# A hybrid decoder on one core: the causal mask of a stick-breaking scan, the order of two PSUM banks and the spacing of the value transposes

## The chip, the cores and the metric

The kernel runs on one core of a Trainium2 chip. The core has a matrix engine (TensorE, in the profile PE, with its weight loads as PEld), three engines for elementwise work (VectorE or DVE, ScalarE or ACT, GpSimd or POOL), a queue (SyncE or SP) that issues the transfers between HBM and the on-chip memory SBUF, and PSUM, eight banks of 128 x 512 fp32 into which PE writes. Each engine runs its own instructions in order and waits on semaphores for the others. The metric is the device time of one launch in microseconds (us), lower is better.

## The reference

Two layers, each a gated pair of attention mixers followed by a convolutional feed-forward block, on 1024 tokens of width 1024, in fp32:

```python
def stick_breaking_attention(q, k, v):
    ...
    def block(args):
        q_blk, i = args
        z = jnp.einsum('bhqc,bhkc->bhqk', q_blk, kt).astype(jnp.float32) * scale
        qpos = i * BLOCK + jnp.arange(BLOCK)
        causal = key_pos[None, :] < qpos[:, None]
        log_stay = jnp.where(causal, jax.nn.log_sigmoid(-z), 0.0)
        later = lax.cumsum(log_stay, axis=3, reverse=True) - log_stay
        attn = jnp.where(causal, jnp.exp(jax.nn.log_sigmoid(z) + later), 0.0)
        return jnp.einsum('bhqk,bhkc->bhqc', attn, vt)
...
def reference(x, norm1, w_in, b_gate, w_br, w_o, norm2, w_up, conv_w, conv_b, w_down, norm_f):
    ...
    for l in range(DEPTH):
        h = rmsnorm(x, norm1[l])
        proj = h @ w_in[l]
        qa, ka, va, qb, kb, vb, gate_pre = jnp.split(proj, splits, axis=-1)
        ...
        o_a = dilated_mixture(hd4(qa, DSW_HEADS), hd4(ka, DSW_HEADS), hd4(va, DSW_HEADS))
        o_b = stick_breaking_attention(hd4(qb, SB_HEADS), hd4(kb, SB_HEADS), hd4(vb, SB_HEADS))
        ...
        merged = g_a * (o_a @ w_br[l, :OUT_A]) + g_b * (o_b @ w_br[l, OUT_A:])
        x = x + merged @ w_o[l]
        h2 = rmsnorm(x, norm2[l])
        ...
        x = x + (jax.nn.gelu(a, approximate=False) * v) @ w_down[l]
    return rmsnorm(x, norm_f)
```

`dilated_mixture` is softmax attention in three head groups (windows of 128, 512 and 2048 tokens, every, every fourth and every sixteenth token). In the stick-breaking part a query attends a key with the sigmoid of its score ("beta"), times the product of one minus that sigmoid ("stay") over all keys between the two. Only keys strictly ahead of the query count.

## The kernel before

**fp32 products.** PE multiplies a reduced form of fp32 (fp32r). An operand is split into a high part (a cast by ACT, L138) and the rest (a subtraction by DVE, L145), and three products of parts are added. Large products are done by blocks with seven instead of eight block products (`seven`, L1001 to L1003): `pair` takes 256 columns of the input projection through weight sums (POOL L1125 and L1134, DVE L1129 and L1135, all on the tile `in_a`), pieces `w_hi` and `w_lo`, and PSUM results `i_a`, `i_c` and `i_b`, which DVE adds up in `u` (L1161, L1167, L1175). After each of four results it calls `put(c, n, ...)`, c being which 128 columns and n which half of the tokens.

**The order.** PE's program is written out by hand: a layer's projection work (`Dense`) and its attention items are recorded in turns. `Dense` yields after each portion, called a share, half of the matmuls of one block product (six); `advance` runs some shares between the steps of attention. `dense.at(n, f)` records f once n more shares have gone by. The other engines' programs are ordered by a scheduler from dependencies and priorities.

**Stick-breaking items.** One item takes 256 queries of one head, as two rows of 128. `score` makes the scores z in PSUM, up to 512 columns at a time; ACT writes beta (L705) and stay (L706, the sigmoid with the sign turned) from them; where a block holds the diagonal, POOL sets the masked part of its last 128 columns, of beta to 0 and of stay to 1 (L709). `scans` runs over stay from the latest key to the earliest with one DVE instruction, a running product (L722: multiply by the next element, then add a column of zeros), and then multiplies beta by it, shifted by one key (L726). The blocks without the diagonal continue from the block behind them. `turn` transposes the result on PE (L734, `sb_t`), ACT and DVE split it (`sbh`, `sbl`), and `apply` multiplies it with the values (L747, `sb_o`). There are 96 scans, of which 64 hold a diagonal. Softmax items work alike: near heads at L638 and L791 to L814, far heads at L859 to L920, whose keys, queries and values are loaded from HBM (`t_kq<-tk`, `slots<-tv`).

**Values.** `pair_v` (L1217 to L1246) projects the values of a head group. Its `put` asks for a turn of the result five shares later: four PE transposes into a bank `v_t` (L1223), the cast by ACT (L1228) and the subtraction by DVE (L1229) into the only buffer of the tile `vv`, and a store to HBM (L1232 or L1234). Successive `put`s are two shares apart. `v_t` shares two PSUM banks (tag "o") with the attention results; `i_a`, `i_b` and `i_c` share another two (tag "ps").

Of the kernel before, what the change touches and what calls it, by code (L numbers as in the profile page):

```python
# [10 lines left out]
BF16 = mybir.dt.bfloat16  # L11
AF = mybir.ActivationFunctionType
ALU = mybir.AluOpType
# [3 lines left out]
P = 128  # L17
# [3 lines left out]
HF = 512  # L21
# [35 lines left out]
def f32(ap):  # L57
    return ap.bitcast(F32)
# [3 lines left out]
def trunk_kernel(ctx, tc, x, norm1, w_in, b_gate, w_br, w_o, norm2, w_up, conv_w, conv_b, w_down, norm_f, out, depth=None, probe=None):  # L62
    nc = tc.nc
    act, dve, pe, pool = nc.scalar, nc.vector, nc.tensor, nc.gpsimd
# [3 lines left out]
    cp = ctx.enter_context(tc.tile_pool(name="cp", bufs=1))  # L68
    sb = ctx.enter_context(tc.tile_pool(name="sb", bufs=1))
    ps = ctx.enter_context(tc.tile_pool(name="ps", bufs=2, space=PSUM))  # L70
# [8 lines left out]
    pool.memset(eps, EPS)  # L79
    zero = cp.tile([P, 1], F32, name="zero")  # L80
    pool.memset(zero, 0.0)
    base0 = cp.tile([P, 256], BF16, name="base0")
    base2 = cp.tile([P, 256], BF16, name="base2")

# [2 lines left out]
    def masks():  # L87

        t = [sb.tile([P, 256], F32, tag="pt", bufs=PT, name=f"msk{i}") for i in range(3)]
        pool.iota(t[1], [[-1, 256]], base=P, channel_multiplier=1, allow_small_or_imprecise_dtypes=True)  # L90
        pool.affine_select(t[1], t[1], [[-1, 256]], ALU.is_ge, FAR, base=P, channel_multiplier=1)
        pool.affine_select(t[2], t[1], [[1, 256]], ALU.is_ge, FAR, base=0, channel_multiplier=-1)
        dve.tensor_copy(base0, t[2])
        rem = sb.tile([P, 256], I32, tag="pt", bufs=PT, name="rem")
        pool.iota(rem, [[-1, 256]], base=256, channel_multiplier=1)
        one = dve.tensor_scalar(rem, rem, 3, None, ALU.bitwise_and)
        tc.add_manual_dep(one.ins, LAST["g0"], NO_SYNC, reason="in turn")
        dve.tensor_copy(t[0], rem)
        dve.tensor_scalar(t[0], t[0], FAR, None, ALU.mult)
        LAST["base"] = dve.tensor_tensor(base2, t[1], t[0], ALU.add).ins.name  # L100
# [18 lines left out]
    sv = [dr.tile([P, n, KD, P], F32, name=f"sv{n}") for n in (4, 2, 2)]  # L119
    dn = [dr.tile([4, T], F32, name=f"dn{i}") for i in range(2)]  # L120

    def bank(tag, name):
        return ps.tile([P, 512], F32, tag=tag, name=name)

    def small(name, dtype=F32):
        return sb.tile([P, 512], dtype, tag="pt", bufs=PT, name=name)
# [510 lines left out]
    def scores(o, qt, ql, k):  # L637
        pe.matmul(o, qt, k, start=True, stop=False, skip_group_check=True)  # L638
        pe.matmul(o, ql, k, start=False, stop=True, skip_group_check=True)
# [48 lines left out]
    def stick_item(dense, u, qp):  # L688
        q, k, v = R["slots"][:, qp], R["kv"][:, 0, :], R["kv"][:, 1, :]
        pr, s = divmod(u, 2)  # L690
        rows, st, shared, left = {}, {}, {}, []

        def score(a):
            L = P * (2 * qp + a + 1)
            bt = rows[a] = sb.tile([P, T], F32, tag="p4", bufs=4, name="beta")
            if a == 0:
                st[0] = sb.tile([P, 2, T], F32, tag="xa", bufs=4, name="stay")
            sv = st[0][:, a, :]
            for c1 in range(L, 0, -512):
                c0 = max(0, c1 - 512)  # L700
                w = c1 - c0
                z = bank("s", "z")
                scores(z[:, :w], *(q[:, x, a * P : a * P + P] for x in range(2)), k[:, c0:c1])
                with tc.high_priority(offset=AHEAD):
                    act.activation(bt[:, c0:c1], z[:, :w], AF.Sigmoid)  # L705
                    act.activation(sv[:, c0:c1], z[:, :w], AF.Sigmoid, scale=-1.0)  # L706
                    if c1 == L:
                        for x, fill in ((bt, 0.0), (sv, 1.0)):
                            pool.affine_select(x[:, L - P : L], x[:, L - P : L], [[-1, P]], ALU.is_gt, fill, base=0, channel_multiplier=1)  # L709
                (SCANS if c1 == L else left).append((shared, bt, sv, c0, c1, L))  # L710
            if a:
                SCANS.extend(left)
                dense.rows += 1
                scans(2)

        def scans(most):

            while SCANS and most:
                most -= 1
                _, bt, sv, c0, c1, L = SCANS.pop(0)  # L720
                rev = sv[:, c0:c1][:, ::-1]
                one = dve.tensor_tensor_scan(rev, rev, zero[:, 0:1].to_broadcast([P, c1 - c0]), 1.0 if c1 == L else sv[:, c1 : c1 + 1], ALU.mult, ALU.add)  # L722
                if "dve" in LAST:
                    tc.add_manual_dep(one.ins, LAST["dve"], NO_SYNC, reason="in turn")
                k0, k1 = max(0, c0 - 1), c1 - 1
                dve.tensor_tensor(bt[:, k0:k1], bt[:, k0:k1], sv[:, k0 + 1 : k1 + 1], ALU.mult)  # L726

        def turn(kb):
            while any(x[0] is shared and x[4] > kb * P for x in SCANS):
                scans(1)  # L730
            tp = bank("t", "sb_t")
            todo = [(j, a) for j in range(2) for a in range(2) if kb + j <= 2 * qp + a]
            for c, (j, a) in enumerate(todo):
                pe.transpose(tp[:, c * P : c * P + P], rows[a][:, (kb + j) * P : (kb + j + 1) * P], ident)  # L734
            shared[kb] = parts(tp, len(todo) * P, "sb")
            scans(2)

        def apply(kb):
            first = kb == 2 * qp
            if first:  # L740
                shared["o"] = bank("o", "sb_o")[:, :256]
                dense.free[qp] = u + 1
            o = shared["o"]
            for j in range(2):
                c = P if first and j else 0
                for p in (0, 1):
                    pe.matmul(  # L747
                        o[:, c:256],
                        v[:, (kb + j) * P : (kb + j + 1) * P],
                        shared[kb][p][:, 256 * j : 256 * j + 256 - c],  # L750
                        start=(first and j == 0 and p == 0),
                        stop=(kb == 0 and j == 1 and p == 1),
                        skip_group_check=True,
                    )
            if kb == 0:
                out_ = small("ob")[0:64, 0:256]
                fold(out_, o)
                nc.sync.dma_start(obd[64 * s : 64 * s + 64, pr, qp * 256 : (qp + 1) * 256], out_)

        sc = [lambda: score(0), lambda: score(1)]  # L760
        return sc, [(lambda kb=kb: turn(kb), lambda kb=kb: apply(kb)) for kb in range(2 * qp, -2, -2)]

# [337 lines left out]
    def pair(dense, l, offs, tiled, put):  # L1100
# [12 lines left out]
        for c in range(2):  # L1113
            one = nc.sync.dma_start(
                raw[:, 2 * c : 2 * c + 2, :].rearrange("p a (k n) -> p (a k) n", n=P),
                w_in[l][:, offs[c] : offs[c] + P].rearrange("(k p) n -> p k n", p=P),
            )
# [20 lines left out]
        u = sb.tile([P, T], F32, tag="wr", bufs=NRAW, name="u")  # L1138
        u1, u2 = u[:, HF:T], u[:, 0:HF]
        u5 = small("u5")  # L1140
        pa, pc = bank("ps", "i_a"), bank("ps", "i_c")
        yield from seven(pa, w1, half(1, 0), True, True)
        yield
        with tc.high_priority(offset=AHEAD):
# [72 lines left out]
    def pair_v(dense, l, g):  # L1217


        def turn(c, n, f):  # L1220
            tp = bank("o", "v_t")
            for r in range(4):
                pe.transpose(tp[:, r * P : (r + 1) * P], f[:, r * P : (r + 1) * P], ident)  # L1223
            tw = tp.rearrange("p (r h c) -> p r h c", r=4, h=2)
            vv = sb.tile([P, 2, 4, P], F32R, tag="ot", name="vv")
            wv = vv.rearrange("p h r c -> p r h c")
            with tc.high_priority(offset=AHEAD):
                act.copy(wv[:, :, :, 0:64], tw)  # L1228
                dve.tensor_tensor(wv[:, :, :, 64:128], tw, f32(wv[:, :, :, 0:64]), ALU.subtract)  # L1229
            if g:  # L1230
                there = tv[c][:, :, :, g - 1, n * P : (n + 1) * P].rearrange("h r p c -> p (h r) c")
                nc.sync.dma_start(there, f32(vv).rearrange("p h r c -> p (h r) c"))  # L1232
            else:
                nc.sync.dma_start(sv[1 + c][:, :, 4 * n : 4 * n + 4, :], f32(vv))  # L1234
            if (c, n) == (1, 1):
                dense.done |= {f"v{g}"} if g else {f"V{u}" for u in range(4, 8)}

        def put(c, n, x, psum, room=None):
            f = x
            if psum:  # L1240
                f = small("vf")
                act.copy(f.rearrange("p (r j) -> p r j", r=4) if g else f, x)
            dense.at(5, lambda: turn(c, n, f))

        off = OFF_VA + 256 * g
        return pair(dense, l, (off, off + P), g > 0, put)  # L1246
# [893 lines left out]
```

## Time and profile before

| | us |
|---|---|
| median of 3 runs | 2643.26 |
| lowest and highest run | 2641.87, 2645.58 |
| the profiled execution | 2641.53 |
| its span, from first to last instruction | 2639.8 |
| PE busy | 2610.7 |
| DVE busy | 2069.4 |
| ACT busy | 1346.8 |
| POOL busy | 685.7 |

How to read it: "L722" is line 722 of the kernel printed above. A timeline row gives the start and the duration in us, the engine, line and operation, what is written from what, the shapes and, in square brackets, how long the engine stood idle just before and what released it. A row with "xN" joins N instructions that follow one another. A row of waits gives "engine, first tile, line <- what ended the wait: total us, times, longest us". A row of a group gives the total busy time, the mean time of one in ns, and after the bar the idle time of the engine just ahead of that group and what ended it. A row of windows gives the window, its length, and then for each engine (PE, PEld, DVE, ACT, POOL) its busy time and the number of instructions, the granted PE clock, the share of the DMA engines and GB/s. Layer 0's attention lies between about 80 and 560 us of the span, layer 1's between about 1380 and 1900.

### The profile page before, as it was taken

Reading aid. Unit: us, or ns where it says so; the run is one execution under the profiler, and the core shown is the slowest. Engines: PE = TensorE matmul, PEld = TensorE weight load, DVE = VectorE, ACT = ScalarE, POOL = GpSimd, SP = SyncE. Lnnn points to the kernel's source line nnn. Section 1 sums busy time; section 2 is a strip of 40 time slices with the busy share of each in tenths; the row PEclk is TensorE's granted clock in tenths of the full one; section 3 lists DMA queues with packets and bytes.
Section 4 is the critical chain, followed back from the end, with each engine's and each line's share of the span. In section 5 each row is a group of like instructions: output and inputs, shape, how many; then the busy total and the mean of one; then the engine's idle time right before and its main releaser. Section 6 shows DMA issues by size and latency. Waiting matters only on the chain.

```text
span 2639.8 us, 36722 instructions
## 1 busy us (share of the span) xinstructions
PE 2610.7 (99%) x12732; PEld 2182.9 (83%) x12732; DVE 2069.4 (78%) x3110; ACT 1346.8 (51%) x2500; POOL 685.7 (26%) x588
## 2 busy tenths in 40 slices
PE   9999999999999999999999999999999999999999
PEld 8888888888888888888888888888888888888887
DVE  7877776785888898896677778677858898888865
ACT  6655566574554555422445555656645555554225
POOL 3222110131143344321222221101321343334200
PEclk9999999999999999999999999999999999999999
DMA  7433587873244444688344436787632444457862
GB/s 253 148 120 128 150 218 197 219 255 88 81 152 149 154 156 148 237 318 315 144 145 144 128 124 174 200 222 217 207 99 82 161 147 156 141 170 259 339 239 111
DMA packets 400423, 468.26 MB, mean 177 GB/s; under 512 B 24309, under 2 KB 315501, under 8 KB 398445
## 3 DMA queue, kind: packets, MB, share of 16 engines
q1 hardware_dynamic: 400220, 465.90, 55.0%
q8 instruction: 101, 1.65, 0.3%
q14 instruction: 86, 0.70, 0.1%
q10 hardware_dynamic: 16, 0.00, 0.0%
HBM read 303.23 MB, written 162.59 MB: 176 GB/s over the span
## 4 chain that ended last, share of the span: by engine, by line
PE 85%; DVE 8%; issue 2%; ACT 2%; DMA 2%; POOL 0%; SPq 0%; DVEq 0%; ACTq 0%; POOLq 0%
PE u_a L1001 5%; PE u_a L1003 5%; PE u_a L1002 5%; PE d_ps L1755 4%; PE d_ps L1757 4%; PE d_ps L1756 4%; PE i_a L1001 4%; PE i_a L1003 4%; PE i_a L1002 4%; PE u_c L1001 3%; PE u_c L1003 3%; PE u_c L1002 3%; PE o_ps L179 2%; PE o_ps L181 2%; PE o_ps L180 2%
## 5 line engine op out<-in xcount | busy, mean ns | idle before, releaser
L145 DVE TENSOR_TENSOR w_lo<-up_a,w_hi 128x512 fp32r<-128x512 f32 x240 | 237.4, 995 | 20.6 <-ACT w_hi L138 20.6
L138 ACT CAST w_hi<-up_a 128x512 fp32r<-128x512 f32 x240 | 149.3, 622 | 184.3 <-PE u_a L1002 45.4
L138 ACT CAST w_hi<-in_a 128x512 fp32r<-128x512 f32 x252 | 156.3, 622 | 159.5 <-PE i_a L1002 58.0
L145 DVE TENSOR_TENSOR w_lo<-in_a,w_hi 128x512 fp32r<-128x512 f32 x252 | 182.8, 727 | 60.9 <-ACT w_hi L138 58.4
L1763 DVE TENSOR_TENSOR x<-x,d_ps 128x512 f32<-128x512 f32 (+1 forms) x228 | 151.9, 671 | 78.2 <-PE d_ps L1757 77.0
L1494 POOL TENSOR_TENSOR cv<-cv 128x512 f32<-128x512 f32 x88 | 132.3, 1515 | 249.6 <-DVE cv L1489 139.8
L145 DVE TENSOR_TENSOR g<-cv,g 128x512 fp32r<-128x512 f32 x154 | 151.9, 988 | 5.2 <-ACT g L138 2.7
L1755 PE MATMUL d_ps<-gd_in,w_hi 128*128 128x512 f32 (+1 forms) x340 | 130.5, 384 | 1.7 <-issue 0.8
L1134 POOL TENSOR_TENSOR in_a<-in_a 128x512 f32<-128x512 f32 x36 | 49.6, 1377 | 314.5 <-DVE w_lo L145 290.2
L1757 PE MATMUL d_ps<-gd_in,w_lo 128*128 128x512 f32 (+1 forms) x340 | 129.8, 382 | 0.0
L1756 PE MATMUL d_ps<-gd_in,w_hi 128*128 128x512 f32 (+1 forms) x340 | 129.8, 382 | 0.0
L1001 PE MATMUL u_a<-hh,w_hi 128*128 128x512 f32 x320 | 124.6, 389 | 0.8 <-DVE u L1645 0.7
L1003 PE MATMUL u_a<-hh,w_lo 128*128 128x512 f32 x320 | 124.5, 389 | 0.0
L1002 PE MATMUL u_a<-hl,w_hi 128*128 128x512 f32 x320 | 124.5, 389 | 0.0
L1001 PE MATMUL u_a<-t_hi,w_hi 128*128 128x512 f32 x320 | 124.5, 389 | 0.0
L1003 PE MATMUL u_a<-t_hi,w_lo 128*128 128x512 f32 x320 | 124.5, 389 | 0.0
L1002 PE MATMUL u_a<-t_lo,w_hi 128*128 128x512 f32 x320 | 124.5, 389 | 0.0
L1001 PE MATMUL i_a<-hh,w_hi 128*128 128x512 f32 x288 | 119.2, 414 | 0.0
L722 DVE TENSOR_TENSOR_SCAN stay<-stay,zero 128x512 f32<-128x512 f32 (+2 forms) x96 | 101.2, 1066 | 22.2 <-POOL stay L709 22.2
L1001 PE MATMUL i_a<-t_hi,w_hi 128*128 128x512 f32 x288 | 118.5, 412 | 0.0
L138 ACT CAST g<-cv 128x512 fp32r<-128x512 f32 x154 | 95.0, 617 | 38.2 <-POOL cv L1494 29.5
L1755 PE MATMUL d_ps<-gd_in,wd 128*128 128x512 f32 (+1 forms) x292 | 113.9, 390 | 0.0
(384 smaller groups left out, 8373.5 us busy)
## 6 DMA issues: line engine op xcount, KB each, us to landing
gd<-g SPq DMA_DIRECT2D x154, 512.0 KB, 3.5
gd_in<-gd SPq DMA_DIRECT2D x154, 512.0 KB, 5.7
up_a<-in_w_up_dram SPq DMA_DIRECT2D x80, 512.0 KB, 4.9
in_a<-in_w_in_dram SPq DMA_DIRECT2D x72, 512.0 KB, 5.6
wd_raw<-in_w_down_dram SPq DMA_DIRECT2D x22, 1024.0 KB, 11.5
gin<-gs SPq DMA_DIRECT2D x32, 512.0 KB, 4.0
w_raw<-in_w_o_dram SPq DMA_DIRECT2D x64, 256.0 KB, 2.9
gs<-u SPq DMA_DIRECT2D x48, 256.0 KB, 3.4
```

What stands on the lines that cost most here:

```text
L138: one = act.copy(hi, src)
L145: two = dve.tensor_tensor(lo, src, f32(hi), ALU.subtract)
L179: pe.matmul(o, lh, rh, start=(first and i == 0), stop=False, skip_group_check=share)
L722: one = dve.tensor_tensor_scan(rev, rev, zero[:, 0:1].to_broadcast([P, c1 - c0]), 1.0 if c1 == L else sv[:, c1 : c1 + 1], ALU.mult, ALU.add)
L1001: pe.matmul(o, w[0][:, c], rh, start=(first and i == 0), stop=False, skip_group_check=True)
L1002: pe.matmul(o, w[0][:, c], rl, start=False, stop=False, skip_group_check=True)
L1003: pe.matmul(o, w[1][:, c], rh, start=False, stop=(last and i == 3), skip_group_check=True)
L1494: return lambda: pool.tensor_tensor(dst, a, b, ALU.subtract)
L1755: pe.matmul(o[:, sub], wh[:, c], gh[:, sub], start=(i == 0 and k in (0, 4, 5)), stop=False, skip_group_check=True)
L1756: pe.matmul(o[:, sub], wh[:, c], gl[:, sub], start=False, stop=False, skip_group_check=True)
L1757: pe.matmul(o[:, sub], wl[:, c], gh[:, sub], start=False, stop=(i == m - 1), skip_group_check=True)
L1763: dve.tensor_tensor(x, x, o[:, sub], ALU.add)
```

## The change

Three edits, none of which changes what is computed:

1. A constant tile `over` of 128 x 512 bf16 is made once: zero, and in its last 128 columns one where the mask applies. Scans of blocks that hold the diagonal take `over` (its last columns, reversed like stay) as their second operand with the maximum in place of the addition, so that the running product is one at masked keys. POOL's select on stay goes; the one on beta remains.
2. In `pair` the PSUM tiles `i_c` and `i_a` are asked for in the other order.
3. The turn of `put(c, n)` comes 4 + c + 2n shares later instead of five: 4, 5, 6 and 7 shares for the four calls, in the order in which they come.

```diff
@@ -79,6 +79,7 @@
     zero = cp.tile([P, 1], F32, name="zero")
     pool.memset(zero, 0.0)
+    over = cp.tile([P, 512], BF16, name="over")
@@ -91,6 +92,8 @@
         dve.tensor_copy(base0, t[2])
+        pool.memset(over, 0.0)
+        pool.affine_select(over[:, HF - P : HF], over[:, HF - P : HF], [[-1, P]], ALU.is_gt, 1.0, base=0, channel_multiplier=1)
         rem = sb.tile([P, 256], I32, tag="pt", bufs=PT, name="rem")
@@ -705,8 +708,7 @@
                     if c1 == L:
-                        for x, fill in ((bt, 0.0), (sv, 1.0)):
-                            pool.affine_select(x[:, L - P : L], x[:, L - P : L], [[-1, P]], ALU.is_gt, fill, base=0, channel_multiplier=1)
+                        pool.affine_select(bt[:, L - P : L], bt[:, L - P : L], [[-1, P]], ALU.is_gt, 0.0, base=0, channel_multiplier=1)
@@ -719,7 +721,10 @@
                 rev = sv[:, c0:c1][:, ::-1]
-                one = dve.tensor_tensor_scan(rev, rev, zero[:, 0:1].to_broadcast([P, c1 - c0]), 1.0 if c1 == L else sv[:, c1 : c1 + 1], ALU.mult, ALU.add)
+                if c1 == L:
+                    one = dve.tensor_tensor_scan(rev, rev, over[:, HF - (c1 - c0) : HF][:, ::-1], 1.0, ALU.mult, ALU.max)
+                else:
+                    one = dve.tensor_tensor_scan(rev, rev, zero[:, 0:1].to_broadcast([P, c1 - c0]), sv[:, c1 : c1 + 1], ALU.mult, ALU.add)
@@ -1138,7 +1143,7 @@
-        pa, pc = bank("ps", "i_a"), bank("ps", "i_c")
+        pc, pa = bank("ps", "i_c"), bank("ps", "i_a")
@@ -1240,7 +1245,7 @@
-            dense.at(5, lambda: turn(c, n, f))
+            dense.at(4 + c + 2 * n, lambda: turn(c, n, f))
```

## The prediction

> **What bounds the kernel now.** I read the page's totals first, then the waits of TensorE (PE), then the groups of the lines that the diff touches, and last the timeline around each PE stall that such a line can reach.
>
> ```profile
> span 2639.8 us, 36722 instructions
> PE 2610.7 (99%) x12732; PEld 2182.9 (83%) x12732; DVE 2069.4 (78%) x3110; ACT 1346.8 (51%) x2500; POOL 685.7 (26%) x588
> ```
>
> PE is busy for 2610.7 of 2639.8 us, so only 29.1 us of the span is idle PE. No edit removes a matmul: the PE program keeps its 12732 instructions. Whatever the change brings must come out of those 29.1 us, and only out of the waits that end on a touched line or on work queued behind one:
>
> ```profile
> PE sb_t L734 <- DVE beta L726: 3.2, 3, 1.7
> PE i_c L1001 <- DVE kq_l L594: 3.0, 2, 1.5
> PE v_t L1223 <- DVE vv L1229: 2.7, 3, 1.7
> ...
> PE z L638 <- DMA slots<-tv: 1.1, 1, 1.1
> ...
> PE z L638 <- DVE st L791: 0.7, 1, 0.7
> ...
> DVE stay L722 <- POOL stay L709: 22.2, 26, 2.0
> ```
>
> The columns are total us, times, longest. The scans' 22.2 us behind Pool's mask look like the prize, but that is idle time of DVE, which is idle for some 570 us anyway; PE pays only where it waits for a scan's successor, L726, or for DVE work queued behind it. The first three rows, 8.9 us, and the last PE row, 0.7 us, are what the edits can reach: 9.6 us is the ceiling of the gain, 0.36% of the span.
>
> **Edit 1, the mask.** It removes 64 Pool selects on stay and makes 64 of the 96 scans read `over` and take the maximum.
>
> ```profile
> L709 POOL TENSOR_SCALAR_AFFINE_SELECT stay<-stay 128x128 f32<-128x128 f32 x64 | 27.1, 423 | 5.1 <-ACT stay L706 4.4
> L722 DVE TENSOR_TENSOR_SCAN stay<-stay,zero x96: 411/1209/2312, 81.0 to 1624.6; 128x512 f32<-128x512 f32 x48, 128x384 f32<-128x384 f32 x16, 128x128 f32<-128x128 f32 x16, 128x256 f32<-128x256 f32 x16
> ```
>
> Pool loses 27.1 us of its 685.7, which no end hangs on. The scan: 411 ns for the narrowest form (128 columns) and about 1209 for 512 give (1209 - 411) / 384 = 2.08 ns a column. The price of `over` in place of a broadcast column is not in the trace. From below: nothing (before, too, the scan reads two operands from SBUF), and no gain, since the number of columns is the same. From above, two nearby rows:
>
> ```profile
> 3.78 0.28 DVE L93 CAST base<-msk 128x256 bf16<-128x256 f32 x1
> ...
> 5.03 0.42 DVE L100 TENSOR_TENSOR base<-msk,msk 128x256 bf16<-128x256 f32 x1
> ...
> 242.13 1.28 POOL L1125 TENSOR_TENSOR in_a<-in_a 128x512 f32<-128x512 f32 x1
> 242.20 2.30 DVE L722 TENSOR_TENSOR_SCAN stay<-stay,zero 128x512 f32<-128x512 f32 x1 [0.54 <-POOL stay L709]
> ```
>
> A second full operand costs (0.42 - 0.28) / 256 = 0.55 ns a column, 0.28 us a 512-wide scan; far out, a scan takes 2.30 us when a Pool tensor_tensor has started just before it, 1.09 more than 1.21. I take nothing: 0.55 ns a column of operand reading fits inside the 2.08 that the scan spends anyway. [...]
>
> Where the earlier start reaches PE, site by site. Site A (twice, once a layer):
>
> ```profile
> 207.11 0.59 ACT L706 ACTIVATE stay<-z 128x512 f32<-128x512 f32 x1
> ...
> 207.77 0.29 POOL L709 TENSOR_SCALAR_AFFINE_SELECT stay<-stay 128x128 f32<-128x128 f32 x1
> ...
> 208.10 1.22 DVE L722 TENSOR_TENSOR_SCAN stay<-stay,zero 128x512 f32<-128x512 f32 x1 [2.01 <-POOL stay L709]
> ...
> 212.89 0.77 DVE L726 TENSOR_TENSOR beta<-beta,stay 128x512 f32<-128x512 f32 x1
> ...
> 213.71 0.44 PE L734 MATMUL sb_t<-ident,beta 128*128 128x128 f32 x2 [0.73 <-DVE beta L726]
> ...
> 1516.61 0.44 PE L734 MATMUL sb_t<-ident,beta 128*128 128x128 f32 x2 [0.73 <-DVE beta L726]
> ```
>
> ScalarE's sigmoid ends at 207.70, the select lets the scan go at 208.06: the scan gains 0.36. From 208.10 to the end of L726 at 213.66 DVE's rows name no idle time, so the whole chain moves: -0.36 of 0.73, twice, -0.7 us. Site D, the third wait for L726:
>
> ```profile
> 1381.26 1.29 POOL L1125 TENSOR_TENSOR in_a<-in_a 128x512 f32<-128x512 f32 x1
> ...
> 1382.59 0.76 DVE L1129 TENSOR_TENSOR in_a<-in_a 128x512 f32<-128x512 f32 x1 [1.45 <-POOL in_a L1125]
> 1383.27 1.30 DVE L722 TENSOR_TENSOR_SCAN stay<-stay,zero 128x512 f32<-128x512 f32 x1
> ...
> 1388.27 0.44 PE L734 MATMUL sb_t<-ident,beta 128*128 128x128 f32 x2 [1.68 <-DVE beta L726]
> ```
>
> Here the built order changes: the scan now stands ahead of L1129, so it may begin while DVE waits for Pool's 1381.26 operation. It then runs beside that operation, as at 242.20, and ends about 1.2 us behind 1382.55, at 1383.8; L1129 follows and the chain behind both is some 0.2 us earlier: -0.2 of the 1.68. Bounds: all 1.68 back, or 1.1 lost.
>
> Site C is a stretch in which DVE never rests, and PE waits at its end:
>
> ```profile
> 277.70:296.40 18.70, 17.22 (x89) 14.08 (x87) 18.70 (x28) 8.01 (x16) 3.83 (x4) 1.00 0.23 87
> ...
> 277.70:296.40 18.70, 5.71 (x6) 1.00 0.23 87
> ...
> 276.87 1.29 POOL L1125 TENSOR_TENSOR in_a<-in_a 128x512 f32<-128x512 f32 x1
> ...
> 277.70 1.01 DVE L145 TENSOR_TENSOR w_lo<-in_a,w_hi 128x512 fp32r<-128x512 f32 x1 [0.95 <-ACT w_hi L138]
> ...
> 291.80 0.68 DVE L145 TENSOR_TENSOR w_lo<-in_a,w_hi 128x512 fp32r<-128x512 f32 x1
> ...
> 296.36 0.50 PE L1001 MATMUL i_c<-t_hi,w_hi 128*128 128x512 f32 x1 [1.48 <-DVE kq_l L594]
> ...
> 1600.07 0.50 PE L1001 MATMUL i_c<-t_hi,w_hi 128*128 128x512 f32 x1 [1.49 <-DVE kq_l L594]
> ```
>
> In the first row, of a window, the third busy time is DVE: 18.70 of 18.70; the second is the same window for L722 alone, six scans. Work that starts no earlier than the window cannot shorten it, but its first operation took 1.01 where the same form takes 0.68, beside Pool's 276.87 operation. Without the stay selects ahead of it Pool starts that operation about 0.6 us earlier and is out of the way: -0.3, in both layers -0.6 us. Bounds: nothing, or the full 3.0.
>
> The new tile costs a Pool memset and select once, at the start.
>
> ```profile
> 405.09 0.52 POOL L857 MEMSET t_kq<- 64x512 f32 x1 [12.97 <-PE o L814]
> ...
> 6.05 0.16 DVE L1976 RECIPROCAL ss<-ss 128x1 f32<-128x1 f32 x1 [0.60 <-ACT ss L1975]
> ```
>
> That is 0.52 plus a 128x128 select of about 0.3; they stand ahead of the mask's iota, whose product DVE uses, and DVE has 0.60 idle before its first work on the path. Nothing; without that cover, 0.8. Edit 1: -1.5 us.
>
> **Edit 2, the banks.** The two tiles share a tag of two banks, and a bank is taken at first use, which is `i_a` in both texts. The built programs with and without this edit are the same in every instruction, wait and bank: nothing, with no bounds to keep.
>
> **Edit 3, the turns.** Four transposes a turn move: first turn a share earlier, second unmoved, third one and fourth two shares later, 24 turns in all. ACT, DVE and one store on SP's queue follow each. Nothing is added. The stall that it is aimed at:
>
> ```profile
> 238.39 0.60 PE L1223 MATMUL v_t<-ident,u 128*128 128x128 f32 x4
> ...
> 242.03 0.60 PE L1223 MATMUL v_t<-ident,u 128*128 128x128 f32 x4
> ...
> 244.96 0.59 ACT L1228 CAST vv<-v_t 128x512 fp32r<-128x512 f32 x1 [0.69 <-DMA sv<-vv]
> ...
> 246.34 0.68 DVE L1229 TENSOR_TENSOR vv<-v_t,vv 128x512 fp32r<-128x512 f32 x1
> ...
> 247.17 0.63 PE L1223 MATMUL v_t<-ident,vf 128*128 128x128 f32 x4 [0.87 <-DVE vv L1229]
> ...
> 1550.85 0.63 PE L1223 MATMUL v_t<-ident,vf 128*128 128x128 f32 x4 [1.66 <-DVE vv L1229]
> ```
>
> The single `vv` buffer holds up ACT until the store before it has landed, DVE empties the bank late, and PE waits in the fourth turn. The second and third turns (238.39 and 242.03) stand two shares apart, so two shares are 3.6 us of PE work, more than either stall: -0.87 - 1.66 = -2.5 us. The third wait on L1229 (2.7 less 2.53: 0.2) and the 0.7 us on L791 lie in one stretch of layer 0,
>
> ```profile
> 409.45 0.39 PE L638 MATMUL z<-kv,slots 128*128 128x256 f32 x1 [0.73 <-DVE st L791]
> ```
>
> where the fourth turn's copy on ACT now falls among `w_hi`, `p0h` and the exponentials: 0.9 freed, 0.6 given back by a 0.59 copy ahead of one of them, -0.3. The moved store on SP goes behind two value loads of the far heads; PE's only wait on such a load (`slots<-tv`, 1.1) is for a later one and stays. Bounds of edit 3: nothing, or -3.4.
>
> **The sum.** -0.7 - 0.2 - 0.6 - 2.5 - 0.3 = -4.3 us. The profiled execution took 2641.53 us, 1.7 outside its span; it would take 2637.2. The median of the runs lies 1.7 above it, so the forecast is 2643.26 - 4.3 = 2638.9 us.
>
> **The rivals.** *More comes free* (26%): DVE's starts ahead of sites C and D move so that their waits go too, -6 to -9.6 us, about 2636. For it: each scan that lost 0.36 at A lost the same elsewhere. Against: site C is full from its first operation. *Edit 3 is absorbed* (12%): the later copies hold up ACT's queue, or the wait on the store turns up at the third turn, which moves one share only; -2.5 and -0.3 go, edit 1 stays: 2641.8. *The second operand is dear* (12%), the one on the slower side: in site C six scans at +1.09, twice, are at most 13.1; at A and D two each, three times, 6.5; less 4.3, so 2643.26 + 15.3 = 2658.6. It decides from about 0.24 us a scan (18 scans, 4.3 us), slightly under the 0.28 of the lower row. Against: both rows are of other operations or of a collision. [...] *It doesn't do what it says*: for edit 2 that is the case, at no cost.
>
> **How the numbers follow.** The forecast has 50%, with its own range of 2637 to 2641. A difference under 0.2%, 5.3 us, can't be told from none here. Faster than 2638.0: the 26% and 6% from the forecast's lower edge, 32%. Slower than 2648.5: the 12%. The rest is no change, 56%. The range runs from 2633 (9.6 under the median, rounded) to 2648, which takes in a scan dearer by up to 0.5 us and leaves out the rival's far end.
>
> **What would show it.** Scans of 128x512 at 1.21 us beside `over`; DVE's wait of 22.2 us on Pool gone, replaced by one on ACT's stay of about half. PE's waits: L726 from 3.2 to about 2.3, kq_l from 3.0 to 2.4, vv from 2.7 to nothing. I am wrong if masked scans show over 1.4 us with no Pool operation beside them, if a PE wait on vv or sbh of over 1 us appears at another turn, or if PE's busy time moves by more than 1 us, since then the span is not made by waits.

## The result and the profile after

| | before, us | after, us |
|---|---|---|
| median of 8 runs | 2642.80 | 2636.35 |
| lowest and highest | 2641.46, 2645.58 | 2635.63, 2637.88 |
| profiled execution (its span) | 2641.53 (2639.8) | 2635.79 (2634.1) |

The ratio is 0.9975, with a 95% interval of 0.9964 to 0.9986: 6.4 us less, where 4.3 were forecast, and the time lies inside the prediction's wide range of 2633 to 2648, but just under the forecast's own, 2637 to 2641.

Behind the change a line number of the text stands one to five lines further down: Pool's select is L711, the scans are L725 (with `over`) and L727, L726 is now L731, L734 is L739, L1223 to L1229 are L1228 to L1234, L594 is L597. First the totals of the page of after:

```profile
span 2634.1 us, 36610 instructions
PE 2609.5 (99%) x12732; PEld 2182.6 (83%) x12732; DVE 2063.8 (78%) x3110; ACT 1346.3 (51%) x2500; POOL 667.3 (25%) x526
```

PE has the same 12732 matmuls and stands idle for 24.6 us instead of 29.1. So 4.5 us of the 5.7 that the span lost are idle time. PE's busy time fell by 1.2 us, although no matmul went. Worked out from the starts and ends of all matmuls, with overlaps counted once, 0.6 us of that belong to the fourth turns (`v_t<-ident,vf`, 3.22 us in before, 2.62 in after): in before, the three of these turns that start behind a stall count for 0.63, 0.66 and 0.63 us, since their first matmul overlaps with nothing before it, where every other turn of either profile counts for 0.44. Another 0.7 is in the 16 matmuls into the tile `warm`, between 1.8 and 8.8 us of the span (3.5 us in before, 2.9 in after).

PE's waits in after (columns as before: total us, times, longest):

```profile
PE i_c L1006 <- DVE kq_l L597: 2.7, 2, 1.4
...
PE u_a L1006 <- DVE u L1650: 2.2, 2, 1.8
PE sb_t L739 <- DVE beta L731: 1.9, 3, 1.2
...
PE z L641 <- DMA slots<-tv: 0.6, 1, 0.6
...
DVE stay L725 <- ACT stay L709: 14.5, 17, 1.6
```

Of the five PE waits that the prediction read, the one for L726 fell from 3.2 to 1.9, the one for kq_l from 3.0 to 2.7, the one on a loaded `slots` from 1.1 to 0.6; those on `vv` (2.7) and on L791 (0.7) are gone. One row grew: `u_a <- u` in the feed-forward block went from 0.7 to 2.2. No edit touches that block. Of the kernels below, the one that keeps the select shows 0.2 for it and all others 1.5 to 2.0, also those that are no faster than the kernel before. Something is given back there; why was not found. DVE's wait ahead of the scans changed its releaser from POOL to ACT and went from 22.2 us to 14.5, two thirds where the prediction had about half.

The scan with the new operand, as the query for its line gives it (ns: shortest, median, longest), and the groups of the select that is left and of the memset that came in (total us, mean ns, idle time before):

```profile
L725 DVE TENSOR_TENSOR_SCAN stay<-stay,over x64: 414/1214/2280, 80.6 to 1618.1; 128x512 f32<-128x512 f32 x40, 128x384 f32<-128x384 f32 x8, 128x128 f32<-128x128 f32 x8, 128x256 f32<-128x256 f32 x8
```

```profile
L711 POOL TENSOR_SCALAR_AFFINE_SELECT beta<-beta 128x128 f32<-128x128 f32 x64 | 30.4, 475 | 265.4 <-ACT beta L708 245.6 <-DVE u L1172 19.7
...
L95 POOL MEMSET over<- 128x512 bf16 x1 | 0.5, 524 | 0.0
```

414 and 1214 ns against 411 and 1209: the operand costs nothing that can be seen. The three sites of edit 1, first A:

```profile
206.84 0.59 ACT L709 ACTIVATE stay<-z 128x512 f32<-128x512 f32 x1
...
207.47 1.22 DVE L725 TENSOR_TENSOR_SCAN stay<-stay,over 128x512 f32<-128x512 f32 x1 [1.64 <-ACT stay L709]
...
213.03 0.44 PE L739 MATMUL sb_t<-ident,beta 128*128 128x128 f32 x2 [0.32 <-DVE beta L731]
```

The scan starts 0.04 us behind the end of the sigmoid (207.43), where it stood 0.40 behind it before, and PE's wait went from 0.73 to 0.32. Site D:

```profile
1377.65 1.29 POOL L1130 TENSOR_TENSOR in_a<-in_a 128x512 f32<-128x512 f32 x1
1377.74 2.28 DVE L725 TENSOR_TENSOR_SCAN stay<-stay,over 128x512 f32<-128x512 f32 x1 [0.21 <-ACT stay L709]
...
1384.23 0.44 PE L739 MATMUL sb_t<-ident,beta 128*128 128x128 f32 x2 [1.24 <-DVE beta L731]
```

The scan, now ahead of L1129, runs into Pool's operation as foretold (2.28 us, where the one at 242.20 before took 2.30 and the median is 1.21) and is still done earlier: 1.68 became 1.24. Site C:

```profile
274.88 1.28 POOL L1130 TENSOR_TENSOR in_a<-in_a 128x512 f32<-128x512 f32 x1
...
276.03 0.69 DVE L148 TENSOR_TENSOR w_lo<-in_a,w_hi 128x512 fp32r<-128x512 f32 x1 [1.28 <-ACT w_hi L141]
...
276.90 0.56 DVE L148 TENSOR_TENSOR sbl<-sb_t,sbh 128x384 fp32r<-128x384 f32 x1 [0.17 <-ACT sbh L141]
...
294.56 0.50 PE L1006 MATMUL i_c<-t_hi,w_hi 128*128 128x512 f32 x1 [1.36 <-DVE kq_l L597]
```

Pool starts 1.15 us ahead of that `w_lo` instead of 0.83, and `w_lo` takes 0.69 instead of 1.01, as was argued. But the wait at the end of the stretch only went from 1.48 to 1.36: the operation behind that `w_lo`, `sbl`, followed it without a gap before and now waits 0.17 us for ACT.

The same matmul of before and after, set beside each other, tells where the 5.7 us of the span come from. The times are those of a matmul behind each stretch:

| stretch | before | after | ahead by | gained here |
|---|---|---|---|---|
| site A, layer 0 (L734) | 213.71 | 213.03 | 0.68 | 0.7 |
| the first group's turns, layer 0 (L1001) | 251.32 | 249.53 | 1.78 | 1.1 |
| far heads begin, layer 0 (L638) | 438.68 | 434.51 | 4.17 | 2.4 |
| site D, layer 1 (L734) | 1388.27 | 1384.23 | 4.04 | -0.1 |
| site A, layer 1 (L734) | 1516.61 | 1512.16 | 4.45 | 0.4 |
| the first group's turns, layer 1 (L1001) | 1555.00 | 1548.66 | 6.34 | 1.9 |
| far heads begin, layer 1 (L638) | 1741.18 | 1734.36 | 6.82 | 0.5 |
| feed-forward block, layer 1 (L1001) | 2047.71 | 2042.72 | 4.99 | -1.8 |

Two rows join stretches in which something was also lost. Ahead of site D the feed-forward block of layer 0 gave back 0.6 us, so that D's own 0.4 doesn't show. In the last row 1.4 of the 1.8 us are lost at the `u_a` matmul itself. One profile has its own accidents, too: ahead of the first attention the profiles of the kernels below lie between 0.4 us behind and 1.4 us ahead of this profile of before, with no pattern by edit. The stretch up to the far heads of layer 0 is the surprise, 2.4 us where the sum had 0.3 for it.

### The profile page after: what moved, and what is told of

Its sections match the earlier page's. It is cut to its first block, busy times and chain, and to the rows that moved or that the text cites. A ratio compares the mean times of both kernels' runs of the same rounds, so it can differ in the third digit from the quotient of the medians.

```text
span 2634.1 us, 36610 instructions
## 1 busy us (share of the span) xinstructions
PE 2609.5 (99%) x12732; PEld 2182.6 (83%) x12732; DVE 2063.8 (78%) x3110; ACT 1346.3 (51%) x2500; POOL 667.3 (25%) x526
## 4 chain that ended last, share of the span: by engine, by line
PE 87%; DVE 8%; DMA 2%; issue 2%; ACT 2%; SPq 0%; POOL 0%; DVEq 0%; ACTq 0%
PE u_a L1006 5%; PE u_a L1008 5%; PE u_a L1007 5%; PE i_a L1006 5%; PE i_a L1007 4%; PE i_a L1008 4%; PE d_ps L1760 4%; PE d_ps L1762 4%; PE d_ps L1761 4%; PE u_c L1008 3%; PE u_c L1006 3%; PE u_c L1007 3%; PE i_c L1006 2%; PE i_c L1007 2%; PE i_c L1008 2%; PE o_ps L182 2%
## 5 line engine op out<-in xcount | busy, mean ns | idle before, releaser
L1008 PE MATMUL i_a<-hh,w_lo 128*128 128x512 f32 x288 | 113.1, 393 | 0.0
```

The lines of the kernel that those rows point to most:

```text
L1008: pe.matmul(o, w[1][:, c], rh, start=False, stop=(last and i == 3), skip_group_check=True)
```

## The experiments

Each was timed in five rounds beside the kernel before on the same chip. Some of the intervals reach 2.4 us to either side, so a single one can't tell a difference of 1 us.

| kernel | median, us | before beside it | ratio | interval |
|---|---|---|---|---|
| mask alone | 2639.23 | 2641.20 | 0.9992 | 0.9983 to 1.0001 |
| turns alone | 2637.41 | 2641.20 | 0.9984 | 0.9975 to 0.9993 |
| mask, select kept | 2641.48 | 2641.20 | 1.0000 | 0.9991 to 1.0009 |
| all turns at seven | 2641.77 | 2641.20 | 1.0002 | 0.9993 to 1.0011 |
| turns of the first group alone | 2638.92 | 2640.63 | 0.9992 | 0.9984 to 1.0001 |
| turns of the two others alone | 2640.91 | 2640.63 | 1.0001 | 0.9992 to 1.0010 |
| changed, four shares apart | 2635.69 | 2640.63 | 0.9982 | 0.9974 to 0.9991 |
| changed, one share later | 2634.97 | 2640.63 | 0.9978 | 0.9969 to 0.9986 |
| mask and first group | 2634.97 | 2641.66 | 0.9977 | 0.9969 to 0.9986 |
| mask and the two others | 2637.77 | 2641.66 | 0.9985 | 0.9976 to 0.9994 |
| the changed kernel again | 2634.76 | 2641.66 | 0.9979 | 0.9970 to 0.9987 |

**The mask alone.** The changed kernel with the old turns:

```diff
-            dense.at(4 + c + 2 * n, lambda: turn(c, n, f))
+            dense.at(5, lambda: turn(c, n, f))
```

> Edit 1 alone (the scan's mask from the constant tile, no select on stay by Pool); turns five shares behind as before. Theory: the mask carries about a third, 1.5 to 2 us (0.7 at the two L726 waits of 0.73, 0.4 at the one of 1.68, 0.3 to 0.6 at the two waits for kq_l), so about 2641 us against 2642.8; the waits of PE on vv, 2.7 us, stay as before. Rival: the turns are what the mask's earlier scans made room for, and the mask alone brings more than half of the 6.4 us: under 2639.5.

2.0 us, the upper end of what the theory said, though the interval takes in zero. Its PE waits:

```profile
PE i_c L1006 <- DVE kq_l L597: 2.8, 2, 1.4
PE sb_t L739 <- DVE beta L731: 2.1, 3, 1.4
...
PE v_t L1228 <- DVE vv L1234: 1.3, 2, 0.8
```

L726 and kq_l nearly as in the changed kernel. One statement failed: the wait on `vv` did not stay, it halved, from 2.7 to 1.3. At the fourth turn of the first group, in layer 1, the timeline has

```profile
1547.49 0.63 PE L1228 MATMUL v_t<-ident,vf 128*128 128x128 f32 x4 [0.83 <-DVE vv L1234]
```

0.83 where it had 1.66. In both layers the `vv` subtraction of DVE stands behind a scan there (in layer 0 the one of 2.30 us at 242.20), and what the mask brings that scan also goes to the turn: in layer 0 DVE idles 0.18 us ahead of it instead of 0.54, the scan takes 2.18 instead of 2.30, and PE waits 0.46 instead of 0.87. Edits 1 and 3 thus overlap in these waits: what one takes the other no longer finds. In the times the overlap does not show: alone they bring 2.0 and 3.8 us, together 6.4 to 6.9.

**The turns alone.**

```diff
-            dense.at(5, lambda: turn(c, n, f))
+            dense.at(4 + c + 2 * n, lambda: turn(c, n, f))
```

> Edit 3 alone (turns three shares apart); Pool masks stay as before. Theory: the greater part, 4 to 5 us, so about 2638.3 us; PE's wait on vv goes (2.7 to 0), and in layer 0 the stretch from 404 to 439 us of the span gains some 2 us more, as in the changed kernel; the L726 waits stay at 3.2. Rival: the third of the gain that the prediction gave to that stretch (0.3) is right for the turns alone and the rest needs the mask: about 2640.3 us.

3.8 us. The wait on `vv` is gone, L726 is at 3.1. Between the matmuls that stand at 251.32 and 438.68 in the profile of before, this kernel's profile gains 2.1 us: the gain in that stretch is there without the mask, and the rival is out for this profile. Some of it comes back as waiting for `t_kq`, 2.3 us against 0.3.

**The select kept.** The mask alone, with Pool masking stay as well:

```diff
-                        pool.affine_select(bt[:, L - P : L], bt[:, L - P : L], [[-1, P]], ALU.is_gt, 0.0, base=0, channel_multiplier=1)
+                        for x, fill in ((bt, 0.0), (sv, 1.0)):
+                            pool.affine_select(x[:, L - P : L], x[:, L - P : L], [[-1, P]], ALU.is_gt, fill, base=0, channel_multiplier=1)
```

> Edit 1 with Pool's select on stay kept (the same values are masked twice): the scan reads the constant tile, but still waits for Pool. Theory: the gain of edit 1 is the wait alone and the second operand costs nothing: the time of the kernel before within 0.5 us, scans of 512 columns at 1.21 us where nothing collides. Rival: the maximum with a bf16 tile is itself cheaper or dearer: more than 1 us from the kernel before, either way.

The time is that of the kernel before, 1.0000, give or take 2.4 us. The group of the masked scans of 512 columns:

```profile
L726 DVE TENSOR_TENSOR_SCAN stay<-stay,over 128x512 f32<-128x512 f32 x40 | 53.1, 1331 | 17.6 <-POOL stay L712 17.6
```

A mean of 1331 ns against 1318 for all 48 of before, and 17.6 us of waiting for Pool against 17.5. The operand is neutral as far as this can tell. What edit 1 brings comes with the select that goes: the scan does not wait for it (site A), and Pool is free earlier (site C). This run does not separate these two.

**Seven shares for all.** The kernel before with the turns later, but no further apart:

```diff
-            dense.at(5, lambda: turn(c, n, f))
+            dense.at(7, lambda: turn(c, n, f))
```

> All four turns seven shares behind their result, two shares apart as before; Pool masks as before. Theory: the distance between turns makes the gain; PE still waits for vv, 2 to 3 us, and the time is that of the kernel before within 1 us. Rival: it is the place of the last turns among the attention items that counts, not their distance; the wait on vv goes and the time comes near to edit 3 alone, 4 us under the kernel before.

The time stayed. PE's wait on `vv` is 1.6 us, below the 2 to 3 expected, but spread over four turns instead of three, and ACT waited 10.3 us for stores of `vv` against 7.6 before. From its waits, and from the query for the tile `vv` (what the copies and stores of it stood idle for: us, times):

```profile
PE v_t L1223 <- DVE vv L1229: 1.6, 4, 0.7
```

```profile
  DMA tv<-vv: 8.0, 5
  DMA sv<-vv: 2.3, 5
```

Turns that are later, but as close, move the waits for the stores to other turns, and the time does not gain: it follows the distance. Place is not without effect, though. At the matmuls of the table above, this profile gains 0.5 and 1.2 us in the first group's two stretches, with the same distance as before. It loses 1.9 us between the far heads of layer 0 and site D, and 2.3 between the first group's turns and the far heads of layer 1; what costs it there was not followed.

**The two parts of edit 3.**

```diff
-            dense.at(5, lambda: turn(c, n, f))
+            dense.at(5 if g else 4 + c + 2 * n, lambda: turn(c, n, f))
```

> Edit 3 in the first head group alone (the two of the six value products that store to sv), the others two shares apart as before; no edit 1. Theory: this holds the two large waits on vv (0.87 and 1.66): 2.5 to 3 us under the kernel before, PE's wait on vv down to the 0.2 of layer 0 at 404 us, and the waits at 409 us (0.73 for L791) and 414 us (0.34 for p0l) as before. Rival: the stretch from 404 to 439 us gains from the first group as well, because everything ahead of it starts earlier: those two waits shrink here too.

1.7 us, under the 2.5 to 3 expected; the waits were as expected (`vv` 0.3, L791 0.7, p0l 0.3), and PE's waiting for `t_kq` rose from 0.3 to 2.8 us. The stretch up to 439 us did not gain, so this rival falls.

```diff
-            dense.at(5, lambda: turn(c, n, f))
+            dense.at(4 + c + 2 * n if g else 5, lambda: turn(c, n, f))
```

> Edit 3 in the two other head groups alone (stores to tv); no edit 1. Theory: in the profile some 2 us come free between 396 and 439 us, since ACT no longer stands at the third turn's copy until the store of the second has landed (1.94 us in the kernel before) with the exponentials and weight casts behind it; the waits at 409 and 414 us go; the two large waits on vv stay (2.5 us); time 1 to 2 us under the kernel before. Rival: no gain here, under 0.5 us, since loads of t_kq that start sooner are waited for instead.

No gain in the runs (1.0001), though in the one profiled execution the stretch between the matmuls at 251.32 and 438.68 came out 1.7 us shorter, near the theory's 2, and the waits at 409 and 414 us were gone. On the measured time it is the rival's number; its reason, the loads of `t_kq`, is not what this profile shows (0.5 us there), but the wait on `vv` that is left grew from 2.7 to 3.3:

```profile
PE v_t L1223 <- DVE vv L1229: 3.3, 2, 2.4
```

**Other distances and places,** both on the changed kernel:

```diff
-            dense.at(4 + c + 2 * n, lambda: turn(c, n, f))
+            dense.at(3 + 2 * c + 4 * n, lambda: turn(c, n, f))
```

> The changed kernel with its turns four shares apart (3, 5, 7 and 9 shares behind). Theory: three shares already keep the copies of a turn clear of the store before (0.8 us of waiting on ACT is left, none on PE), so a fourth brings nothing: within 1 us of the changed kernel, some 2635 to 2636 where the kernel before has 2641 to 2642. Rival: the remaining waits of ACT and the late chain behind the last turn still cost, and it is 1 us or more faster or slower.

```diff
-            dense.at(4 + c + 2 * n, lambda: turn(c, n, f))
+            dense.at(5 + c + 2 * n, lambda: turn(c, n, f))
```

> The changed kernel with each turn one share later (5, 6, 7 and 8 shares behind), three shares apart. Theory: the distance makes the gain and the place does not: within 1 us of the changed kernel, PE does not wait for vv. Rival: the place among the attention items matters, and a wait on vv, sbh or p0l of 0.5 us or more comes back.

0.9982 and 0.9978 against 0.9975 and 0.9979 for the changed kernel: no difference that can be told, and PE waits for `vv` in neither. Four shares apart, ACT no longer waits for any store of `vv` at all (0.8 us in the changed kernel), and that brings nothing; one share later it waits 5.2 us for them, and that costs nothing. Three shares are enough, and where they begin does not matter within a share, as far as these intervals can tell.

**The parts together with the mask,** the changed kernel with one part of the turns put back, and the changed kernel beside them:

```diff
-            dense.at(4 + c + 2 * n, lambda: turn(c, n, f))
+            dense.at(5 if g else 4 + c + 2 * n, lambda: turn(c, n, f))
```

> The changed kernel with the turns of the second and third head group put back to five shares. Theory: the terms add; mask 2.0 and first group 1.7 give 3.7 us under the kernel before, and the turns of the other two groups are worth the remaining 2 us of the changed kernel, those that its profile shows between 396 and 439 us; here the waits for L791 at about 405 us (0.7) and for p0l (0.3) are back. Rival: the other two groups bring nothing that lasts to the end (they measured 1.0001 alone): within 0.8 us of the changed kernel on the same chip.

```diff
-            dense.at(4 + c + 2 * n, lambda: turn(c, n, f))
+            dense.at(4 + c + 2 * n if g else 5, lambda: turn(c, n, f))
```

> The changed kernel with the turns of the first head group put back to five shares. Theory: 1.7 us above the changed kernel, or less, since the mask alone has halved the wait on vv (2.7 to 1.3); that wait shows here at the first group's fourth turn, about 1 us. Rival: 0.5 us or less above it, because the mask frees DVE early enough in that stretch.

> The changed kernel itself beside the other two on the same chip. Every theory: 0.9975 to 0.998 of the kernel before, as measured before; it is the base from which the two parts are counted.

Without the turns of the two other groups the kernel is as fast as with them, 2634.97 against 2634.76, and the waits for L791 and p0l are not back: the rival holds. Without the first group's it is 3.0 us slower, more than expected, and PE waits for `vv` again:

```profile
PE v_t L1228 <- DVE vv L1234: 2.2, 2, 1.7
```

The eight kernels in which each of the three parts is either in or out, by their distance to the kernel before beside them, are: none 0; mask -2.0; first group -1.7; other groups +0.3; mask and first -6.7; mask and others -3.9; both groups -3.8; all -6.9. The mean of the four with a part less the mean of the four without it is -3.6 us for the mask, -3.4 for the first group and -1.0 for the others. With some 2.4 us to either side of each of the seven measured numbers, and their errors taken as independent, I estimate 1.6 us to either side of these means: the first two are clear of zero, the third is not. The parts do not simply add up. Mask and first group bring 2.0 and 1.7 alone and 6.7 together, more than the sum; on top of the other groups' turns they bring 4.2 and 4.1 alone and 7.2 together, less than the sum. With this noise it stays open whether the two help or hinder each other.

**What the other groups' turns do.** In the kernel before, the third turn of that stretch waits on ACT for the store of the second:

```profile
397.51 5.17 DMA tv<-vv
```

```profile
402.78 0.59 ACT L1228 CAST vv<-v_t 128x512 fp32r<-128x512 f32 x1 [1.94 <-DMA tv<-vv]
...
404.33 0.40 ACT L792 ACTIVATE p<-p,st 128x128 f32<-128x128 f32 x1 [0.96 <-DVE st L791]
...
409.43 0.51 ACT L792 ACTIVATE p<-p,st 128x256 f32<-128x256 f32 x1 [0.72 <-DVE st L791]
```

The first row is from the chain of waits, the others from the timeline. The store took 5.17 us to land, and the exponentials come behind the copy that waits for it. In the profile of "mask and first group", with the turns of this stretch two shares apart as before, the same store landed in 2.9 us and the copy waited for nothing (a row of its timeline, one of the query for `vv` between 390 and 415 us, one of its PE waits):

```profile
398.09 0.59 ACT L1233 CAST vv<-v_t 128x512 fp32r<-128x512 f32 x1
```

```profile
DMA to landing us min/median/max: 2.9/2.9/2.9
```

```profile
PE z L641 <- DMA t_kq<-tk: 3.3, 2, 1.8
```

The store took 5.1 to 5.3 us in the profiles of the kernel before, the mask alone, the select kept and the first group alone, 2.9 in this one. In this one PE got 2.0 us further ahead of the kernel before between 394 and 436 us, with turns as close as there, and gave back 1.5 of them at the far heads; the last row shows that, 3.3 us of waiting for their keys and queries. So part of what three shares gain in this stretch hangs, by this one profile, on how long the store happens to take. Why its landing differs was not found.

In the profiles as a whole these turns do gain there: between the matmuls at 251.32 and 438.68 the five kernels with them three shares apart from the fourth share on (changed kernel twice, turns alone, others alone, mask and others) gain 1.7 to 2.5 us, and four with them as before (mask alone, select kept, first group alone, mask and first) between -0.5 and 0.6. That this is not seen at the end, 0.2 us between mask and first group and the changed kernel, has no explanation here.

## Why the prediction was right, and where its terms were off

**The number.** The forecast had the direction, the ceiling and most of the sites right, and 4.3 of the 6.4 us. The interval of the ratio, 3.7 to 9.5 us, holds 4.3. Still, 2636.35 is under the forecast's own 2637 to 2641, and 6.4 us lies in the band of the rival *More comes free*, 6 to 9.6. Of the terms, the stretch of layer 0 in edit 3 was far too small for the profile (0.3 against 2.4), site C was too large (0.6 against 0.2 to 0.3), and what ends the two large stalls on `vv` was misread, at no cost to the sum (below, at edit 3).

**The bound.** The gain did come out of PE's idle time, 4.5 of 5.7 us in the profile, and stayed under the ceiling of 9.6. The prediction's own alarm, that PE's busy time moves by more than 1 us, went off with 1.2; half of it, 0.6, is in the fourth turns behind stalls, so the reading of the span as made by waits stands, with that half added to the idle time.

**Edit 1, -1.5 forecast.** Alone 2.0, over the eight kernels 3.6 give or take 1.6. Its three sites together came out at 1.5 us, as summed, by luck: D gave what C fell short. Site A: 0.41 in layer 0, 0.36 forecast. Site D: 0.44 against 0.2, by the mechanism described, with the collision (the scan of 2.28 us). Site C: Pool's earlier start and the shorter `w_lo` came as forecast, the wait shrank by 0.12 instead of 0.3: the step "-0.3, in both layers" failed in size. Of the 0.32 us that `w_lo` lost, `sbl` behind it starts only 0.07 earlier, as ACT's `sbh` ends just before it; another 0.08 come from an L726 that took 0.77 us beside a select and now takes 0.68. That DVE was full from the window's first operation did not show that ACT stood so close behind. The term that was missing here is the first group's turns: the mask alone takes 1.4 us off the waits on `vv`, which the sum had put down to edit 3 only; in the total it was counted. The operand's price of nothing, the choice with the widest bounds, is shown twice, by the 1214 ns and by the kernel with the select kept; the rival "the second operand is dear" is refuted. Why it costs nothing no run shows: that 0.55 ns of reading a column fit inside the 2.08 of the scan was the author's estimate. The rival's price was set too high, too: of the six scans counted in site C only two read `over`, the other four belong to blocks without the diagonal. The start costs nothing that can be told: the memset took 0.52 us on Pool, as the row that stood for it.

**Edit 2.** That it does nothing rests on the two programs being the same; no run has it alone, so it is not shown.

**Edit 3, -2.8 forecast.** Alone 3.8. The two large stalls are gone, and the stretches around them gained 1.1 and 1.9 us, 3.0 where the sum had 2.5. But the step "the single `vv` buffer holds up ACT until the store before it has landed, DVE empties the bank late" is not what ended last at these two. In the kernel before, DVE's rows ahead of the subtraction that empties the bank, in layer 0 (the scan of 2.30 us at 242.20 comes just before them), and ACT's copy and that subtraction in layer 1:

```profile
244.53 0.69 DVE L726 TENSOR_TENSOR beta<-beta,stay 128x511 f32<-128x511 f32 x1
245.14 0.68 DVE L145 TENSOR_TENSOR sbl<-sb_t,sbh 128x512 fp32r<-128x512 f32 x1
245.74 0.68 DVE L145 TENSOR_TENSOR w_lo<-in_a,w_hi 128x512 fp32r<-128x512 f32 x1
...
1545.87 2.31 DVE L722 TENSOR_TENSOR_SCAN stay<-stay,zero 128x512 f32<-128x512 f32 x1 [0.66 <-POOL stay L709]
...
1548.61 0.59 ACT L1228 CAST vv<-v_t 128x512 fp32r<-128x512 f32 x1 [1.44 <-DMA sv<-vv]
...
1550.02 0.68 DVE L1229 TENSOR_TENSOR vv<-v_t,vv 128x512 fp32r<-128x512 f32 x1
```

The copy that had waited for the store ended at 245.55 and at 1549.20, 0.8 us before DVE began the subtraction (246.34 and 1550.02), and from the slow scan up to that subtraction DVE's rows name no idle time. So DVE's queue behind a scan that ran beside Pool (2.30 and 2.31 us) kept the bank, and the store at most indirectly: in layer 1 it held up the copy of the turn before by 0.67 us, ahead of that scan. This is also why the mask alone halves these stalls. The bank came free 5.0 and 5.8 us after the transposes into it began, and PE was ready for the next turn after 4.3; in the changed kernel it is free after 2.0 and 2.3 us, and the next turn comes after 6.0. The store does end the wait last in layer 0 between 396 and 404 us. That distance makes the gain is borne out by the seven shares for all, which brought nothing in time, and by the two other sets of places at three and four shares, which kept it. The term "0.9 freed, 0.6 given back, -0.3" for the stretch of layer 0 was mis-sized for this profile: 2.4 us came free in it. The 0.6 to be given back at ACT did not show in it, and the prediction had counted only the 0.9 of stalls that stand at a touched line, not what else comes behind ACT's 1.94 us of waiting. But over many runs the turns of the two groups that lie there are worth 1.0 give or take 1.6, and 0.2 on top of the rest: a forecast of 0.3 for the median is not refuted.

**The rivals.** "More comes free" named the mechanism of sites C and D and a time of 2636, and the time came close to it, by another way: C barely moved, and D's wait shrank by 0.44 of its 1.68. "Edit 3 is absorbed" is refuted, 3.8 us for the turns alone. The wait on `slots` stayed, smaller (0.6), as the prediction said that it would stay.

## What to carry to other kernels

Where one engine is busy 99% of the time, list its waits and add up only those that end on touched lines: the 22.2 us that another engine waited were worth 2 to 4 here. For a buffer that is emptied late, follow each engine that empties it back to its last idle time: here the wait for the store was in plain sight on ACT, and a full DVE ended 0.8 us later. Once the distance between uses is clear of that time, more distance and another place bring nothing that these runs can tell. And two edits that relieve the same stall from two sides are neither to be added up nor to be measured only one at a time.

## What was not expected of the hardware

The same store of `vv` landed in 2.9 us in some profiles and in 5.1 to 5.3 in others; in the kernel before, the DMA engines' share was 0.84 of the two us from 398 to 400 and 0.08 of the two after, so the store landed, at 402.68, behind a long tail with the engines all but idle:

```profile
398.00:400.00 2.00, 2.00 (x13) 1.69 (x13) 0.97 (x3) 0.53 (x2) 0.00 (x0) 1.00 0.84 255
400.00:402.00 2.00, 2.00 (x14) 1.76 (x13) 0.69 (x1) 0.84 (x2) 0.00 (x0) 1.00 0.08 16
```

The longest selects of Pool are those that start just behind the start of a scan: the six longest of those left, 0.96 to 1.21 us where the median is 0.29, start 0.21 to 0.35 us after a scan does, the longest of them after one of 1.33 us. The kernel before had this too (its six longest, 0.90 to 1.07 us, start 0.23 to 0.40 us after one). The mean rose from 429 to 475 ns, and no wait of PE ends on one.
